# First modulation in two halves, and new instruction costs in the planner, for a two-layer hybrid-mixer and experts kernel

## The chip, the cores and the metric

The kernel runs on one core of a Trainium2 chip. The metric is the device time of one launch in microseconds (us); the time before is the median of three runs, 1281.8 us (1279.6 to 1284.72).

A core has TensorE (matrix products into PSUM), VectorE, ScalarE, GpSimd and SyncE. Each works through its own list of instructions in order and waits for the others by semaphores. In the profile they are PE (with PEld for the loading of a matmul's stationary operand), DVE, ACT, POOL and SP. SP here issues nearly all loads of weights.

## The reference, cut to what matters

The input is 512 tokens of width 1024; there are two layers. Every layer is modulated by six vectors (shift, scale and gate, twice) that come from one condition vector `c`:

```python
mod_all = einsum('bd,lde->lbe', silu(c), ada_w) + ada_b[:, None, :]
for l in range(2):
    sh1, sc1, g1, sh2, sc2, g2 = split(mod_all[l][:, None, :], 6, axis=-1)
    h = rms_norm(x, norm_mix_g[l]) * (1.0 + sc1) + sh1
    proj = h @ w_in[l]
    # four mixers of width 256 each, all fed from columns of proj:
    mix = concat([nsa(...), pool(...), rwkv7(...), dilated(...)])
    x = x + g1 * (mix @ w_out[l])
    h2 = rms_norm(x, norm_ffn_g[l]) * (1.0 + sc2) + sh2
    x = x + g2 * moe(h2)          # 16 experts, two per token
```

`ada_w` is 2 x 1024 x 6144 in float32, so one of the six vectors of one layer costs 4 MB of weights, multiplied with a single column.

## The kernel before, in words

**Modulation.** The 512 columns of half a vector, by four pieces of 256 rows, are one unit of 512 KB each (eight units to a vector). `ada_s` is the stream of these units in the order in which they are used: for layer 0 scale (v = 1), then shift (v = 0), then the rest. `ada` multiplies them: `zc` holds silu(c) as one column in a band of zeros, so that a matmul with a 32-column window of `zc` as stationary operand puts its result in row j = 2v + jj of a 32-row group (jj is the half of the vector). Four groups run side by side on TensorE, and VectorE adds all rows to `MT`, where the bias already stands (L667). `mcol` (L726) then takes rows of `MT` and turns them into columns: entry k of `A1` and `B1` is what contraction tile k of the projection is scaled and shifted by, and tiles 0 to 3 come from half 0, tiles 4 to 7 from half 1.

**The head of layer 0.** The tokens are loaded, their square sums taken (`rms`, two ScalarE passes for each of the four row tiles, L797), each row scaled by its norm, and the eight tiles of 128 columns transposed on TensorE and copied from PSUM to `hf` by ScalarE (L873, L881). Then SP is told to load the 16 units of scale and shift and two units of the projection's weights, and the main program waits for `ada` as a whole. After that follow the affine of all eight tiles (L900 on ScalarE for odd tiles, L902 on VectorE for even ones), their split into a rounded part `hH` (L903, ScalarE) and the rest `hL` (L905, VectorE), and the projection.

**Products.** Every large product is made of three matmuls in a rounded 32-bit form: high by high, high by low and low by high (`mm3`, L603 to L605). Weights are split in the same way (`split`, L555 on ScalarE and L556 on VectorE) by the streams' `presplit`, one or more units ahead. The projection runs by chunks of columns, `c0`, `c1`, `c2`, `t0`, `t1`, `t2`; a chunk takes four weight units u, each of which covers contraction tiles 2u and 2u + 1. Chunk `c0` has four column tiles, so a unit is 24 matmuls of 512 columns.

**Order.** The program is written as generators: a main one (the projections, the output projection, the experts) and side ones (the recurrent mixer, attention, pooling, modulation, routing). `_Weaver` interleaves them while the instructions are emitted, by the forecasts of `_Clock`, a small model of the engines that runs along: `cost` gives each instruction a time, `see` adds waits for data from other engines (`SEM`, 130 ns), `pass_time` forecasts TensorE's two clock levels. A side's next step is emitted once its forecast of readiness plus a lead is before TensorE's forecast time. `W.pace` sets lead and share for each stage (`PROJ`, `ATT`, `WOUT`, `MOE`). So the forecast decides in which order instructions stand on every engine, in both layers, and on the chip each engine then keeps to that order. A step that a `yield side` asks for is emitted at once, ready or not.

**Buffers.** 39 buffers of 512 KB (`G`) hold tokens, raw and split weights and most intermediate tiles; SP's loads wait until a buffer is free. PSUM has four buffers in pool `PA` and four in `PB`.

Of the kernel before, what the change touches and what calls it, by code (L numbers as in the profile page):

```python
# [210 lines left out]
class _Clock:  # L211
# [5 lines left out]
    def __init__(self, nc):  # L217
        self.free = {}
        self.acc = {}
        self.pools = {}  # L220
        self.psum = set()
        self.dma = self.mark = 0.0
        self.off = False
        self.tick, self.cols, self.cold = 0.0, 0.0, True
        self.batch, self.batch_end = set(), 0.0
        nc.push_inst_callback(self.see)
# [29 lines left out]
    @staticmethod  # L256
    def cost(eng, inst, psum):
        o = inst.outs[0]
        shape = [int(n) for _, n in o.ap]
        n = 1  # L260
        for x in shape[1:]:
            n *= x
        if eng == "PE":
            i0 = inst.ins[0]
            if inst.is_transpose:
                return 0.84 * n
            if i0.dtype == F32R and n >= 256 or i0.dtype == BF:
                return max(0.42 * n, 25.0)
            return 1.67 * max(n, shape[0])
        if eng == "DVE":  # L270
            return 65 + 1.04 * n
        if eng == "Activation":
            return (94 if psum else 180) + 0.833 * n + (94 if len(inst.outs) > 1 else 0)
        if "TensorScalar" in str(inst.opcode):
            return 100 + 3.7 * n
        return 70 + (2.25 if len(inst.ins) > 1 else 1.0) * n
# [12 lines left out]
    def see(self, inst):  # L289
        if self.off:  # L290
            return
        try:
            outs = [o for o in inst.outs if hasattr(o, "bass_ap")]
            ins = [i for i in inst.ins if hasattr(i, "bass_ap")]
            if not outs:
                return
            eng = str(inst.engine).split(".")[-1]
            rd, wr = [self.region(i) for i in ins], [self.region(o) for o in outs]
        except (AttributeError, TypeError, ValueError):
            return  # L300
        t = self.free.get(eng, 0.0)
        mine = t
        for regs, write in ((rd, False), (wr, True)):
            for name, p0, p1, lo, hi in regs:
                for q0, q1, l2, h2, end, w, by in self.acc.get(name, ()):
                    if (write or w) and by != eng and q0 < p1 and p0 < q1 and l2 < hi and lo < h2:
                        if end > t:
                            t = end
        if "DMA" in str(inst.opcode):
            self.free[eng] = mine + (1000.0 if eng == "Pool" else 50.0)  # L310
            sizes = [4 * float(np.prod([int(n) for _, n in x.ap])) for x in outs + ins]
            self.dma = max(self.dma, t + 1300.0) + min([z for z in sizes if z > 16384] or sizes) / 360.0
            end = self.dma + 500.0
        else:
            c = self.cost(eng, inst, bool(rd) and rd[0][0] in self.psum)
            if eng == "PE":
                m, q0 = int(outs[0].ap[0][1]), wr[0][1]
                kr, r0 = int(inst.ins[0].ap[0][1]), rd[0][1]
                qs = {(a, b) for a in range(r0 // 32, (r0 + kr + 31) // 32) for b in range(q0 // 32, (q0 + m + 31) // 32)}
                small = m <= 64 or kr <= 64  # L320
                self.pass_time(t)
                slow = 2 if self.cold and HAM else 1
                c *= slow
                if not small or qs & self.batch or t >= self.batch_end:
                    t = max(t, self.batch_end)
                    self.batch = qs
                    self.batch_end = t + c
                    more = c
                    if small:
                        more = min(c, 0.84 * m * slow)  # L330
                else:
                    self.batch |= qs
                    self.batch_end = max(self.batch_end, t + c)
                    more = 0.84 * m * slow
                n = 1
                for _, x in inst.outs[0].ap[1:]:
                    n *= int(x)
                n *= 1 if inst.ins[0].dtype != F32 else 2 if inst.is_transpose else 4
                self.pass_time(t + c / 2, n * int(inst.ins[0].ap[0][1]) / 128)
                self.free[eng] = t + more  # L340
            else:
                self.free[eng] = t + c
            end = t + c + self.SEM
        self.mark = max(self.mark, end)
        for regs, write in ((rd, False), (wr, True)):
            for name, p0, p1, lo, hi in regs:
                lst = self.acc.setdefault(name, [])
                if write:
                    lst[:] = [a for a in lst if not (p0 <= a[0] and a[1] <= p1 and lo <= a[2] and a[3] <= hi)]
                lst.append((p0, p1, lo, hi, end, write, None if "DMA" in str(inst.opcode) else eng))  # L350
                if len(lst) > 60:
                    del lst[:20]
        self.log[inst.name] = (t, end) if self.log is not None else None
# [86 lines left out]
def fused(ctx: ExitStack, tc: tile.TileContext, A, out, dbg=None):  # L440
# [31 lines left out]
    def TI(name, w=64, dt=F32):  # L472
        return tip.tile([128, w], dt, name=name, tag="ti")

    def PA(name):
        t_ = pa.tile([128, 512], F32, name=name, tag="a")
        K.alloc("a", NPA, t_)
        return t_
# [162 lines left out]
    def mod_rows(l):  # L641
        GP.memset(MT, 0.0)
        GP.dma_start(MT[0:12], A["ada_b"][l])
        if l + 1 < L:
            GP.dma_start(MT[12:16], A["ada_b"][l + 1, 0:4])


    ada_s = Stream([(A["ada_w"][l, 2 * v + jj, u], 512) for l, v in
                    [(0, v) for v in (1, 0, 2, 4, 3, 5)] + [(1, v) for v in (1, 0, 2, 4, 3, 5)]
                    for jj in range(2) for u in range(4)], 3, raw=True)  # L650

    def ada(l, vs, more=True):
        if more:
# [146 lines left out]
    def rms(xt, n=NT):  # L800
        ms = TI("ms", n)
        for t in range(n):
            square(xt[t], ms[:, t:t + 1])
        V.tensor_scalar(ms, ms, 1.0 / D, EPS, op0=OP.mult, op1=OP.add)
        rs_ = TI("rs_", n)
        rsqrt(ms, rs_, n)
        return rs_
# [38 lines left out]
    def layer(l, xt, mixs, moes, nmixs):  # L846
# [23 lines left out]
        def transposed(k):  # L870
# [2 lines left out]
                PE.transpose(tp[:, t * 128:(t + 1) * 128], xt[t][:, k * 128:(k + 1) * 128], ident)  # L873
            return tp

        if l == 0:
            mc = PA("mc")
            A1, B1 = TI("A1", 8), TI("B1", 8)
            for k in range(8):
                tp = transposed(k)  # L880
                SC.activation(hf[k // 2][:, k % 2], tp, AF.Copy)  # L881
            ada_s.cap = 16
            ada_s.load(16)
            mixs.load(2)
            yield W.spawn(ada(0, [(0, 1), (0, 0)], False))
            mcv = mcol(mc, 0, 4)
            V.scalar_tensor_tensor(qj(A1), mcv[:, :, 2:4], 1.0, qj(col("gmix", 0, 8)), op0=OP.add, op1=OP.mult)
            V.tensor_copy(qj(B1), mcv[:, :, 0:2])
        else:
            A1, B1 = P_.A1, P_.B1  # L890
        parts = [(hH[k // 2][:, k % 2], hL[k // 2][:, k % 2]) for k in range(8)]
        late = None
        for k in range(8):
            if l == 0:
                src = f_ = hf[k // 2][:, k % 2]
            else:
                src = transposed(k)
                f_ = HG("hf1")
            if k % 2:
                SC.activation(f_, src, AF.Identity, scale=A1[:, k:k + 1], bias=B1[:, k:k + 1])  # L900
            else:
                V.tensor_scalar(f_, src, A1[:, k:k + 1], B1[:, k:k + 1], op0=OP.mult, op1=OP.add)  # L902
            SC.activation(parts[k][0], f_, AF.Copy)  # L903
            if late:
                V.tensor_tensor(late[2], late[0], late[1].bitcast(F32), op=OP.subtract)  # L905
            late = (f_,) + parts[k]
        V.tensor_tensor(late[2], late[0], late[1].bitcast(F32), op=OP.subtract)
        hH = [hH[k // 2][:, k % 2] for k in range(8)]
        hL = [hL[k // 2][:, k % 2] for k in range(8)]
        yield  # L910
# [2 lines left out]
        def cchunk(name, evac):  # L913
            n = len(CHUNKS[name])
            ps = [PA(name) for _ in range(n // 128)]
            for u in range(4):
                wh, wl = mixs.get()
                for c in range(n // 128):
                    cs_ = slice(c * 128, (c + 1) * 128)
                    for i in range(2):  # L920
                        k = 2 * u + i
                        mm3(ps[c], wh[:, i, cs_], wl[:, i, cs_], hH[k], hL[k], k == 0, k == 7)
                    if u == 3:
                        evac(c, ps[c])
                    yield
# [1353 lines left out]
```

## Time and profile before

| what | value |
|---|---|
| median of 3 runs | 1281.8 us |
| the profiled execution | 1281.02 us, span 1279.2 us |
| mean granted TensorE clock | 0.933 of full speed |
| TensorE busy | 1096.8 us, 86% of the span |
| VectorE busy | 873.5 us, 68% |
| ScalarE busy | 587.3 us, 46% |
| GpSimd busy | 161.7 us, 13% |
| read from HBM | 213.76 MB |

The span is what the profile covers; the execution's own time is 1.8 us longer. Busy time is the union of an engine's instructions. A granted clock of 1.00 is 2.4 GHz, 0.50 is 1.2 GHz. In the trace one float32 matmul of the modulation has two records. Layer 0 lies between 0 and about 637 us, layer 1 behind it.

### The profile page before, as it was taken

How to read it: one execution, taken by the hardware profiler on the slowest of the kernel's cores; microseconds unless marked ns; L12 is line 12 of the kernel's file. 1: busy time of each engine (PE TensorE's matmuls, PEld its weight loads, DVE VectorE, ACT ScalarE, POOL GpSimd, SP SyncE). 2: the span in 40 equal slices, each digit the busy share in tenths (PEclk: the TensorE clock that was granted, in tenths of full speed). 3: DMA queues.
4: the chain of work that ended last, by engine and by line, in shares of the span. 5: the costliest groups of instructions: out<-in, count | busy, mean ns of one | idle time of the engine just before them, and what ended most of it. 6: DMA issues, size and time to landing. Idle time of an engine off the chain costs nothing. (4 is left out here: it accounts for less than half of the span.)

```text
span 1279.2 us, 21615 instructions
## 1 busy us (share of the span) xinstructions
PE 1096.8 (86%) x8150; PEld 822.5 (64%) x8150; DVE 873.5 (68%) x2200; ACT 587.3 (46%) x1088; POOL 161.7 (13%) x140
## 2 busy tenths in 40 slices
PE   4699999978999579999749879998888994899995
PEld 2487678545778467777538557784476783667774
DVE  2538866666655679999852665955685465899994
ACT  4433222346672156666551411243376431666662
POOL 2000000100001222233200000001000022213331
PEclk9799999989899789999969989998978996999998
DMA  9502111956351869999351110047431428699982
GB/s 353 191 33 83 34 37 40 348 208 258 116 182 55 332 207 323 334 351 358 116 193 35 50 67 35 21 141 274 169 121 57 158 73 324 231 326 343 353 290 37
DMA packets 68320, 232.05 MB, mean 181 GB/s; under 512 B 10580, under 2 KB 11460, under 8 KB 68208
## 3 DMA queue, kind: packets, MB, share of 16 engines
q1 hardware_dynamic: 54960, 192.18, 41.1%
q0 software_dynamic: 10368, 27.92, 7.9%
q10 hardware_dynamic: 2880, 10.49, 2.2%
q8 instruction: 67, 1.10, 0.3%
q14 instruction: 45, 0.37, 0.1%
HBM read 213.76 MB, written 25.17 MB: 187 GB/s over the span
## 5 line engine op out<-in xcount | busy, mean ns | idle before, releaser
L556 DVE TENSOR_TENSOR wl<-raw,wh 128x1024 fp32r<-128x1024 f32 (+2 forms) x254 | 299.7, 1197 | 38.3 <-ACT wh L555 35.3
L555 ACT ACTIVATE wh<-raw 128x1024 fp32r<-128x1024 f32 (+2 forms) x254 | 251.0, 1038 | 14.0 <-DMA raw<-w_out 8.1
L603 PE MATMUL gu<-wh,eh 128*128 128x512 f32 x256 | 104.8, 409 | 0.0
L605 PE MATMUL gu<-wh,el 128*128 128x512 f32 x256 | 102.6, 401 | 2.4 <-DVE el L556 1.4
L604 PE MATMUL gu<-wl,eh 128*128 128x512 f32 x256 | 101.4, 396 | 0.0
L555 ACT ACTIVATE eh<-etp 128x512 fp32r<-128x512 f32 x64 | 35.0, 595 | 114.3 <-PE etp L2039 98.5
L603 PE MATMUL c<-hH,wh 128*128 128x512 f32 x176 | 71.2, 405 | 10.7 <-ACT wh L555 10.7
L603 PE MATMUL t<-wh,hH 128*128 128x512 f32 (+1 forms) x192 | 79.9, 416 | 0.0
L604 PE MATMUL t<-wl,hH 128*128 128x512 f32 (+1 forms) x192 | 71.2, 371 | 7.8 <-DVE wl L556 7.8
L605 PE MATMUL c<-hH,wl 128*128 128x512 f32 x176 | 69.9, 397 | 2.4 <-DVE wl L556 2.4
L605 PE MATMUL t<-wh,hL 128*128 128x512 f32 (+1 forms) x192 | 70.7, 368 | 0.0
L604 PE MATMUL c<-hL,wh 128*128 128x512 f32 x176 | 69.6, 396 | 0.0
L1610 ACT ACTIVATE P<-P,mx 128x128 f32<-128x128 f32 (+3 forms) x96 | 52.7, 550 | 34.1 <-DVE mx L1607 33.9
L603 PE MATMUL dp<-wh,ahl 128*128 128x512 f32 x128 | 54.2, 423 | 15.1 <-ACT ahl L555 15.1
L605 PE MATMUL dp<-wh,ahl 128*128 128x512 f32 x128 | 54.0, 422 | 12.8 <-DVE ahl L556 12.8
L1285 POOL TENSOR_SCALAR sd<-st,pcs 128x64 f32<-128x64 f32 x28 | 10.8, 398 | 409.5 <-DVE st L1309 317.6
L605 PEld LDWEIGHTS gu<-wh,el 128*128 128x128 f32 x256 | 48.8, 191 | 17.8 <-DVE el L556 7.1
L1629 PE MATMUL ptp<-cbase,P 128*128 128x128 f32 x240 | 44.0, 314 | 15.2 <-ACT P L1622 7.7
L664 PE MATMUL ada<-raw,zc 128*32 128x512 f32 x384 | 55.1, 631 | 0.9 <-DMA raw<-ada_w 0.9
L604 PEld LDWEIGHTS gu<-wl,eh 128*128 128x128 f32 x256 | 49.2, 192 | 9.3
L603 PEld LDWEIGHTS gu<-wh,eh 128*128 128x128 f32 x256 | 49.1, 192 | 9.1 <-ACT eh L555 0.5
L2007 POOL DMA_INDIRECT ga<-h2d,idx x32 | 46.5, 1454 | 61.6 <-DVE dtw L1906 17.7
(591 smaller groups left out, 2376.0 us busy)
## 6 DMA issues: line engine op xcount, KB each, us to landing
raw<-w_gu SPq DMA_DIRECT2D x120, 512.0 KB
raw<-ada_w SPq DMA_DIRECT2D x96, 512.0 KB
raw<-w_dn SPq DMA_DIRECT2D x60, 512.0 KB
raw<-win_c SPq DMA_DIRECT2D x16, 512.0 KB
raw<-win_t SPq DMA_DIRECT2D x16, 512.0 KB
raw<-w_out SPq DMA_DIRECT2D x16, 512.0 KB
x<-x SPq DMA_DIRECT2D x8, 512.0 KB
h2d<-h SPq DMA_DIRECT2D x8, 512.0 KB
```

The source lines that it names most:

```text
L555: SC.activation(h_, src, AF.Copy)
L556: eng.tensor_tensor(l_, src, h_.bitcast(F32), op=OP.subtract)
L603: PE.matmul(o, lhsT=sh, rhs=mh, start=first, stop=False)
L604: PE.matmul(o, lhsT=sh, rhs=ml, start=False, stop=False)
L605: PE.matmul(o, lhsT=sl, rhs=mh, start=False, stop=last)
L664: PE.matmul(ps[g:g + 32], lhsT=zc[:, k, 31 - j:63 - j], rhs=raws[i // 2][:, i % 2], start=u2 == jj == 0, stop=u2 == jj == 1)
L1285: GP.tensor_scalar(sd[:, i * 64:(i + 1) * 64], st[c][:, i * 64:(i + 1) * 64], pcs[i][:, c:c + 1], 0.0, op0=OP.mult, op1=OP.add)
L1610: SC.activation(P[:, par, :n], P[:, par, :n], AF.Exp, scale=-1.0, bias=mx[:, par:par + 1], accum_out=den[:, par:par + 1])
L1629: PE.transpose(tp[:, ks_], P[:, par, ks_], ident)
L2007: GP.indirect_dma_start(out=g_, out_offset=None, in_=h2d, in_offset=bass.IndirectOffsetOnAxis(ap=info[e][0], axis=0))
```

## The change

Three things are changed. The first is the planner's costs: matmuls, ScalarE and VectorE operations get other times; an operation on VectorE or ScalarE that reads what the same engine has written waits for that write's end plus `SEM`; VectorE and GpSimd operations that read two tensors from SBUF exclude each other; a change of a matmul's tile shape costs 93 ns. The leads and shares stay.

The second is the head of layer 0. The stream `ada_s` delivers half 0 of scale and shift first, then half 1. `ada_first(jj)` multiplies one half, and `cols(jj)` makes its four columns of `A1` and `B1`. Half 0 stands in the main program: three of its four matmul groups, then the transposes of tiles 0 to 3, the split of the first weight unit, the fourth group, the columns, and the affine and split of tiles 0 to 3, in between the transposes of tiles 4 to 7. Half 1 with tiles 4 to 7 is a side, `upper`, and chunk `c0` asks for it ahead of its third unit. The copies of odd transposed tiles go to VectorE.

The third is `rms` in the head: the square sums of row tiles 1 and 3 are taken on VectorE, in one pass of 1024 columns each.

```diff
 # _Clock.cost
-                return max(0.42 * n, 25.0)
-            return 1.67 * max(n, shape[0])
+                return max(0.445 * n, 25.0)
+            return (2.05 if shape[0] <= 32 and n > 128 else 1.72) * max(n, shape[0])
         if eng == "DVE":
-            return 65 + 1.04 * n
+            return 65 + 1.04 * n + (60 if len([i for i in inst.ins if hasattr(i, "bass_ap")]) > 2 else 0)
         if eng == "Activation":
-            return (94 if psum else 180) + 0.833 * n + (94 if len(inst.outs) > 1 else 0)
+            more = len([i for i in inst.ins if hasattr(i, "bass_ap") and "const" not in i.bass_ap.tensor.name]) > 1
+            return (70 if psum else 94) + 0.833 * n + 93 * more + (93 if len(inst.outs) > 1 else 0)
...
 # _Clock.see
-                    if (write or w) and by != eng and q0 < p1 and p0 < q1 and l2 < hi and lo < h2:
+                    if (write or w) and (by != eng or w and not write and eng in ("DVE", "Activation")) and q0 < p1 and p0 < q1 and l2 < hi and lo < h2:
...
+        two = sum(r[0] not in self.psum for r in rd) > 1 and "DMA" not in str(inst.opcode)
+        if eng == "DVE" and two:
+            t = max(t, self.lock["Pool"])
+        if eng == "Pool" and two:
+            t = max(t, self.lock["DVE"])
...
+                if form != self.form:
+                    self.batch_end += 93
...
+    def ada_first(jj):
+        ps = PB("ada")
+        for v in (1, 0):
+            j = 2 * v + jj
+            for u2 in range(2):
+                raws = [ada_s.get() for _ in range(2)]
+                K.mark = max(K.last(r_.tensor.name) for r_ in raws)
+                yield
+                for i in range(4):
+                    g, k = 32 * i, 4 * u2 + i
+                    PE.matmul(ps[g:g + 32], lhsT=zc[:, k, 31 - j:63 - j], rhs=raws[i // 2][:, i % 2],
+                              start=v == 1 and u2 == 0, stop=v == 0 and u2 == 1)
+        V.tensor_tensor(MT, MT, ps, op=OP.add)
...
 # rms
-            square(xt[t], ms[:, t:t + 1])
+            if t % 2:
+                V.tensor_tensor_reduce(G("jk"), xt[t], xt[t], 1.0, 0.0, op0=OP.mult, op1=OP.add,
+                                       accum_out=ms[:, t:t + 1])
+            else:
+                square(xt[t], ms[:, t:t + 1])
...
 # head of layer 0
+            def raise_(k):
+                tp = transposed(k)
+                if k % 2:
+                    V.tensor_copy(hf[k // 2][:, k % 2], tp)
+                else:
+                    SC.activation(hf[k // 2][:, k % 2], tp, AF.Copy)
+
+            def cols(jj):
+                mcv = mcol(PB("mc"), 0, 4)
+                hs_ = slice(4 * jj, 4 * jj + 4)
+                V.scalar_tensor_tensor(A1[:, hs_], mcv[:, :, 2 + jj], 1.0, col("gmix", 4 * jj, 4), op0=OP.add, op1=OP.mult)
+                V.tensor_copy(B1[:, hs_], mcv[:, :, jj])
+
+            def upper_half():
+                yield from ada_first(1)
+                cols(1)
+                yield
+                yield from part_of(range(4, 8))
+
             ada_s.cap = 16
-            ada_s.load(16)
-            mixs.load(2)
-            yield W.spawn(ada(0, [(0, 1), (0, 0)], False))
-            mcv = mcol(mc, 0, 4)
...
+            ada_s.load(8)
+            mixs.load(2)
+            ada_s.load(12)
+            mixs.load(3)
+            ada_s.load(16)
+            mixs.load(4)
+            steps = ada_first(0)
+            for _ in range(4):
+                next(steps)
+            for k in range(4):
+                raise_(k)
+            mixs.presplit(1)
+            for _ in steps:
+                pass
+            cols(0)
+            for k, _ in enumerate(part_of(range(4)), 4):
+                raise_(k)
+            upper = W.spawn(upper_half(), front=True, lead=0)
...
 # cchunk
                 wh, wl = mixs.get()
+                if u == 2 and upper is not None:
+                    yield upper
```

`part_of(ks)` is the former loop over tiles (affine, high part, low part one tile later) for the tiles `ks`, with a `yield` after each.

## Rows read from the trace of the kernel before

**Rows 1.** Busy time by stretch: start:end, length, busy us (instructions) by engine, clock, DMA, GB/s.
```profile
0.00:46.00 46.00, 17.53 (x105) 8.69 (x106) 15.50 (x62) 21.96 (x42) 8.26 (x19) 0.91 0.95 355
...
100.00:250.00 150.00, 145.81 (x1557) 109.43 (x1556) 107.78 (x314) 43.09 (x84) 2.95 (x6) 0.99 0.28 101
250.00:372.00 122.00, 107.56 (x1030) 70.93 (x1026) 76.13 (x305) 71.16 (x202) 3.62 (x10) 0.90 0.55 198
...
454.00:637.00 183.00, 166.74 (x879) 127.54 (x877) 168.78 (x260) 119.32 (x160) 52.10 (x29) 0.98 0.83 288
...
700.00:750.00 50.00, 40.08 (x179) 26.79 (x179) 31.49 (x76) 19.19 (x28) 0.00 (x0) 0.95 0.18 61
...
870.00:1004.00 134.00, 112.08 (x1033) 77.36 (x1025) 82.93 (x328) 74.60 (x208) 4.67 (x12) 0.87 0.42 144
```

**Rows 2.** Timeline of the head: start, us, engine, line, operation [idle before <-releaser].
```profile
17.79 5.09 PE L873 MATMUL tp<-cbase,x 128*128 128x128 f32 x30 [0.35 <-ACT x L865]
...
22.81 6.13 PE L664 MATMUL ada<-raw,zc 128*32 128x512 f32 x48
...
31.73 1.05 PE L664 MATMUL ada<-raw,zc 128*32 128x512 f32 x4 [0.23 <-DMA raw<-ada_w]
...
33.01 1.05 PE L664 MATMUL ada<-raw,zc 128*32 128x512 f32 x4 [0.23 <-DMA raw<-ada_w]
34.11 0.69 DVE L667 TENSOR_TENSOR mt<-mt,ada 128x512 f32<-128x512 f32 x1 [6.82 <-PE ada L664]
...
34.85 1.05 PE L726 MATMUL mc<-cbase,mt 128*128 128x4 f32 x8 [0.79 <-DVE mt L667]
...
36.30 0.55 DVE L902 TENSOR_SCALAR hf<-hf,A,B 128x512 f32<-128x512 f32 x1
...
38.90 1.29 DVE L905 TENSOR_TENSOR hL<-hf,hH 128x512 fp32r<-128x512 f32 x2 [0.22 <-ACT hH L903]
...
45.57 0.80 PE L603 MATMUL c<-hH,wh 128*128 128x512 f32 x1 [9.67 <-ACT wh L555]
```

**Rows 3.** Busy time by stretch of 2 us in the head.
```profile
18.00:20.00 2.00, 2.00 (x11) 2.00 (x11) 0.00 (x0) 1.19 (x2) 0.00 (x0) 1.00 1.01 406
...
36.00:38.00 2.00, 0.00 (x0) 0.00 (x0) 1.20 (x4) 1.12 (x2) 0.00 (x0) 1.00 1.04 408
38.00:40.00 2.00, 0.00 (x0) 0.00 (x0) 1.78 (x4) 1.97 (x4) 0.00 (x0) 0.54 1.01 404
```

**Rows 4.** Timeline of TensorE, the first projection matmuls.
```profile
51.26 0.63 PE L603 MATMUL c<-hH,wh 128*128 128x512 f32 x1
51.69 0.46 PE L604 MATMUL c<-hL,wh 128*128 128x512 f32 x1
...
52.22 0.39 PE L603 MATMUL c<-hH,wh 128*128 128x512 f32 x1
...
59.70 0.39 PE L603 MATMUL c<-hH,wh 128*128 128x512 f32 x1
```

**Rows 5.** Groups by line and form: out<-in xcount | busy us, mean ns | idle before.
```profile
L556 DVE TENSOR_TENSOR wl<-raw,wh 128x1024 fp32r<-128x1024 f32 x238 | 286.1, 1219 | 24.7 <-ACT wh L555 21.7
L555 ACT ACTIVATE wh<-raw 128x1024 fp32r<-128x1024 f32 x238 | 239.2, 1056 | 14.0 <-DMA raw<-w_out 8.1 <-DMA raw<-w_gu 3.3 <-issue 2.4
...
L1633 DVE COPY pt<-ptp 128x512 f32<-128x512 f32 x12 | 8.2, 687 | 3.4 <-PE ptp L1629 3.4
```

**Rows 6.** Timeline of VectorE: two operations, the second reads the first's result.
```profile
726.47 0.68 DVE L996 TENSOR_TENSOR df<-vfirst,zv 128x512 f32<-128x512 f32 x1
727.19 0.69 DVE L997 TENSOR_TENSOR df<-df,vrs 128x512 f32<-128x512 f32 x1
```

**Rows 7.** Timeline of TensorE: first output projection, layer 1's first projection and output projection.
```profile
372.11 0.50 PE L603 MATMUL wo<-wh,mH 128*128 128x512 f32 x1
...
663.89 0.47 PE L603 MATMUL c<-hH,wh 128*128 128x512 f32 x1
...
1003.93 0.50 PE L603 MATMUL wo<-wh,mH 128*128 128x512 f32 x1
```

## The prediction before the run

> **What bounds the kernel now.** I read the times and the page first, then the table of busy time by stage, then the timeline of the head, then the waits of TensorE. The table by stage [rows 1] shows four kinds of stretch. In the head (0 to 46 us) TensorE works 17.5 of 46 us while the DMA share is 0.95: the loads set the pace. In the projections TensorE is nearly full. In the attention stretches (250 to 372, 870 to 1004) it loses 14.4 and 21.9 us to waits, and its mean granted clock is 0.90 and 0.87. In the experts (454 to 637) VectorE works 168.8 of 183 us and the DMA share is 0.83, so TensorE is not the only bound there.
>
> The change's hand-made part lies in the head. Its timeline [rows 2] is a chain: the last raw piece of `ada_w` lands, its matmuls start at 33.01, VectorE adds the result to `mt` at 34.11, the column matmuls start at 34.85, the first affine at 36.30, and the first projection matmul only at 45.57, after 9.67 us in which TensorE did nothing. The last two waiting groups stand 1.28 us apart (31.73, 33.01): one 512 KB piece per 1.28 us. The projection then starts at half clock: the granted clock falls from 1.00 (36 to 38 us) to 0.54 (38 to 40 us) [rows 3], and matmuls come 0.43 us apart (51.26, 51.69), after that 0.227 us (33 of them from 52.22 to 59.70) [rows 4]. The first two weight units of chunk c0 (48 matmuls, contraction tiles 0 to 3) end where the 49th matmul starts, at 59.70.
>
> **The change, part by part.** All sums are against the profiled execution's 1281.0 us (span 1279.2); the median shown is 1281.8, so 0.8 is added at the end.
>
> *Loads.* Lower-half pieces of both vectors come first (8), then two weight units, four upper pieces, one unit, four upper, one unit. Counting 1.28 us back from 33.01, the eighth piece lands at 22.8 as it does now; the first weight unit at 24.1; the last upper piece, behind three weight units that now precede it, at 33.0 + 3 x 1.28 = 36.8. The bytes are the same, the queue (SP's) is the same; so upper modulation data come 3.8 us later than now and lower data 10.2 us earlier than the whole does now.
>
> *Lower chain.* Three of the four lower matmul groups stand ahead of the first transposes on TensorE, so the transposes wait for the sixth piece (20.2) plus 1.05: 21.3. Now 30 transposes take 5.1 us [rows 2], 0.68 per tile of four, held by ScalarE's copies; with every second copy on VectorE (a copy of that shape 0.69 [rows 5]) I take 0.6 per tile: 23.7 for four tiles. The fourth group adds 1.06 (48 records in 6.13 us [rows 2], 8 per group): 24.8. The add to `mt` stands behind the low split of weight unit 0 on VectorE: unit 0 lands 24.1, ScalarE's high part 1.06, VectorE's low part 1.22 [rows 5], so the add starts at 26.3 and ends at 27.0. Column matmuls 1.1, A and B 0.36 (34.85 to 36.30 [rows 2], less the wait): first affine at 28.5. Now the high and low parts of tiles 0 and 1 are there some 3.3 us after the first affine (36.30; the second and third low parts start 38.90 [rows 2]); the copies of the upper transposes lie between them, one on ScalarE and one on VectorE, so I take 4.0: 32.5. The square sum of rows 1 and 3 moves to VectorE: two passes over 128x1024, at most about 1.22 each [rows 5], on an engine that waits there anyway; TensorE starts its transposes on pieces, not on the norm, so it gains and costs nothing. Without that cover it would cost 2.4.
>
> *Both units of the lower half.* 48 matmuls at 0.227 are 10.9 us, of which three may run before 32.5: 42.7. Two upper groups land before 32.5 (pieces at 26.6 to 30.5) and fit into the wait; two more fall in between, 2.1 us. The second add and the second column matmuls are new waits in TensorE's order: 1.05 for the columns, 0.69 for the add and up to 1.2 for a split queued ahead of it on VectorE; queued behind the columns on TensorE are the remaining c0 matmuls, which everything later waits for. I take 2.5. Sum 47.3. The upper chain, if its last group is placed soon after 36.8, has tiles 4 and 5 by about 45.8, so it doesn't end last. The third unit starts at about 47.5 instead of 59.70: **12 us gained.** Bounds: 14 if all stalls vanish (45.5), 3 if the last upper group is placed at the end of the second unit (the chain of 4.5 us is then open) and the first unit runs at half clock (24 x 0.2 = 4.8). The rope tables, a side on VectorE, share the stretch; I leave them in the 2.5.
>
> *Does the shift reach the end?* The matmuls from 52.22 on have no gap [rows 4], TensorE works 145.8 of 150 us from 100 to 250, the DMA share there is 0.28 [rows 1], and all later loads are released by buffers that TensorE frees. Nothing in the first 400 us waits for an absolute time, so I carry the 12 us through.
>
> *The planner's new costs.* They change no instruction but the order of nearly all of them, in both layers. What they correct is visible: a 512-column matmul is forecast at 0.215 (0.42 per column) and takes 0.227 [rows 4]; two VectorE operations where the second needs the first start 0.72 apart [rows 6] and were forecast at 0.60. Late forecasts of VectorE put work too early in TensorE's order, and TensorE then stands: idle 4.2, 14.4, 9.9 and 21.9 us in 100 to 250, 250 to 372, 700 to 750 and 870 to 1004 [rows 1], 50 us together. The leads and shares, which were set under the old forecast, stay. Best case: half of the 50 goes, -25. Worst case: the trace holds two orders of nearly the same work. From the first projection matmul to the first of the output projection layer 0 takes 372.1 - 45.57 = 326.5 and layer 1 takes 1003.93 - 663.89 = 340.0 [rows 2, 7]; part of the 13.5 is extra work of layer 1, so it is an upper bound of what an order is worth, for two layers 27. Between -25 and +27 I take -3, near nothing: the correction points the right way, its size isn't shown. The lock between VectorE and GpSimd hardly matters where GpSimd works 3 us of 150 [rows 1].
>
> Sum: 1281.0 - 12 - 3 = 1266.0; with 0.8 for the median **1267 us**.
>
> *A rule against it.* The granted clock is 1.00 during the transposes (18 to 20 us) and still from 36 to 38, and falls after TensorE has had no instruction since 35.9 [rows 2, 3]. The Trainium skill says of transposes ("TensorE: Matmul & The Clock Gate", Part 4: PE-mode transpose) that they do not count as busy for the clock the way matmuls do. The order after has 32 transposes with only short matmul groups between 21 and 31 us, so by that rule the first lower unit would meet the half clock; no run here yet shows it, since now a dense matmul group follows the transposes at once. What this would cost is the rival "half clock" below.
>
> **Rivals.**
> - *Half clock.* The lower units start at 0.43 per matmul. For it: sparse matmuls between 21 and 32 us. Against it: the groups paced by the loads, 1.05 us in 1.28, left the clock at 1.00 until 36 to 38 us [rows 2, 3]. At 14 slow matmuls as now [rows 4] 2.8 us are lost, at all 48 it is 9.6 us: 1270 to 1276.
> - *The wait moves.* The upper chain ends last at the third unit, because its add and splits queue on VectorE or its last group is placed late. For it: VectorE has splits, rope and both adds there. 4 to 6 us of the 12 remain: 1273 to 1275.
> - *The order takes it all* (the other side). The new forecasts make side work be issued later, the unchanged leads then come too late, and TensorE waits more in projections and attention of both layers. It decides from 6 us per layer on. At 13.5 per layer: 1281.8 - 12 + 27 = 1297. For it: nothing else in the planner was set anew. Against it: the new costs are nearer to the rows.
> - *The order gives much.* Half of TensorE's 50 us of waits go: 1281.8 - 12 - 25 = 1245.
> - *The halves do nothing*: the lower part is forced behind the upper in TensorE's order, no gain in the head, 1279.
>
> **Numbers.** The forecast (1260 to 1273) 0.42; half clock 0.10; the wait moves 0.08; the order gives much 0.16; head gain eaten to within measurement 0.14, of it the idle halves 0.03; order takes more 0.10. A measurement of this kernel tells changes above some 0.5%, 6.4 us. Faster: 0.42 + 0.10 + 0.08 + 0.16 = 0.76; same 0.14; slower 0.10. Low end 1249: three quarters of "gives much" is inside. High end 1283: it holds the two late rivals and the eaten gain, and leaves out the slower cases. The likeliest case's own range is 1260 to 1273.
>
> **What would show it.** Right: the first c matmul before 33 us, the 49th at 46 to 49, its wait under 2 us; the last `ada` matmul at about 37 to 39; granted clock 1.00 from 24 to 50; two `mt` adds, near 26.5 and 40. Wrong in the head: a TensorE wait of over 3 us ended by VectorE (`hL`, `mt`) before the 49th matmul, or 0.43 us spacing. The planner's part is read from the same two intervals, 326.5 and 340.0: taken from the 49th c matmul on in layer 0, and whole in layer 1. If the second moves by over 10 us either way, the -3 was the failed step; if the experts' stretch moves by over 5, the carry-through was.

## The result and the profile after

The change ran in 1260.55 us (median of four runs, 1255.66 to 1272.69) against 1280.7 us before (1279.08 to 1284.72): a ratio of 0.9859, 95% interval [0.9821, 0.9897], or 18 us (13 to 23). A second measurement of the same kernel, among the experiments, gave 1257.09 us and 0.9809 [0.9784, 0.9833]. The forecast was 1267, with 1249 to 1283 as its range.

The profiled execution is the longest of the four (1272.69 us), so it understates the gain. Its page, part 1: busy time, share of the span, instructions.

```profile
span 1270.9 us, 21609 instructions
...
PE 1106.8 (87%) x8158; PEld 822.9 (65%) x8158; DVE 874.7 (69%) x2208; ACT 581.7 (46%) x1076; POOL 167.6 (13%) x140
```

TensorE is busy 10 us longer than before, with eight more records (the second set of column matmuls) and no lower mean clock (0.935 against 0.933). What differs is how much of its work meets the half clock: counted from the trace, 114 us of TensorE's busy time fall into half clock, against 102 before, where more of the half clock fell into waits. The second profile below (69 us) shows the same order with less of it.

The head, timeline of the changed kernel (columns as in [rows 2], which it answers):

```profile
23.40 1.06 PE L677 MATMUL ada<-raw,zc 128*32 128x512 f32 x8
...
25.39 1.23 DVE L569 TENSOR_TENSOR wl<-raw,wh 128x1024 fp32r<-128x1024 f32 x1 [1.19 <-ACT wh L568]
26.53 0.68 DVE L679 TENSOR_TENSOR mt<-mt,ada 128x512 f32<-128x512 f32 x1
...
27.27 1.87 PE L755 MATMUL mc<-cbase,mt 128*128 128x4 f32 x8 [2.81 <-DVE mt L679]
...
29.00 3.65 PE L906 MATMUL tp<-cbase,x 128*128 128x128 f32 x16
...
29.44 0.55 DVE L923 TENSOR_SCALAR hf<-hf,A,B 128x512 f32<-128x512 f32 x1
...
34.14 0.50 PE L616 MATMUL c<-hH,wh 128*128 128x512 f32 x1
34.48 0.39 PE L617 MATMUL c<-hL,wh 128*128 128x512 f32 x1
34.71 0.39 PE L618 MATMUL c<-hH,wl 128*128 128x512 f32 x1
...
42.26 1.07 PE L677 MATMUL ada<-raw,zc 128*32 128x512 f32 x8
43.41 0.69 DVE L679 TENSOR_TENSOR mt<-mt,ada 128x512 f32<-128x512 f32 x1 [3.88 <-PE ada L677]
...
44.16 1.05 PE L755 MATMUL mc<-cbase,mt 128*128 128x4 f32 x8 [0.84 <-DVE mt L679]
```

The lower chain runs as forecast: the add to `mt` at 26.53 (forecast 26.3), the first affine at 29.44 (28.5). The first projection matmul starts at 34.14 instead of 45.57. Then TensorE's own timeline:

```profile
50.64 0.39 PE L616 MATMUL c<-hH,wh 128*128 128x512 f32 x1
...
51.32 0.39 PE L616 MATMUL c<-hH,wh 128*128 128x512 f32 x1
53.71 0.50 PE L617 MATMUL c<-hL,wh 128*128 128x512 f32 x1 [2.00 <-DVE hL L926]
...
54.72 0.63 PE L617 MATMUL c<-hL,wh 128*128 128x512 f32 x1
55.14 0.63 PE L618 MATMUL c<-hH,wl 128*128 128x512 f32 x1
```

The matmul at 50.64 is the 49th of chunk c0 (59.70 in [rows 4]). Four matmuls later TensorE waits 2.0 us for the low part of tile 5, and the next nine or so come at half clock. The 96th, the last of c0, starts at 65.2 against 70.4 before: of the 9.1 us at the 49th, 5.2 are left.

**Two runs of one order.** A second profile of the changed kernel (experiment e4) has the same instructions in the same order, took 1256.07 us, and starts its instructions from 20 to 27 us within 0.05 us of the first one's (0.4 us before); behind that they part. Its head, timeline of TensorE:

```profile
27.22 1.05 PE L755 MATMUL mc<-cbase,mt 128*128 128x4 f32 x8 [2.81 <-DVE mt L679]
28.14 1.94 PE L906 MATMUL tp<-cbase,x 128*128 128x128 f32 x16
30.33 1.07 PE L677 MATMUL ada<-raw,zc 128*32 128x512 f32 x8 [0.25 <-ACT hf L938]
31.33 0.50 PE L616 MATMUL c<-hH,wh 128*128 128x512 f32 x1
```

The wait of 2.81 us is the same; but the column matmuls take 1.05 and not 1.87 us, the transposes 1.94 and not 3.65, and the projection starts at 31.33. Busy time by stretch (columns as in [rows 3]), first the run above, then e4:

```profile
24.00:26.00 2.00, 0.46 (x8) 0.00 (x0) 0.81 (x2) 1.06 (x1) 0.00 (x0) 1.00 1.05 418
26.00:28.00 2.00, 0.73 (x4) 0.73 (x4) 1.21 (x2) 0.00 (x0) 0.00 (x0) 0.74 1.00 401
28.00:30.00 2.00, 2.00 (x11) 2.00 (x11) 0.78 (x3) 0.00 (x0) 0.00 (x0) 0.50 1.05 416
```
```profile
26.00:28.00 2.00, 0.78 (x7) 0.78 (x8) 1.17 (x2) 0.00 (x0) 0.00 (x0) 1.00 1.02 408
28.00:30.00 2.00, 2.00 (x19) 1.84 (x18) 0.95 (x4) 0.84 (x2) 0.00 (x0) 1.00 1.04 410
```

In the long run the granted clock fell to 0.50 during that wait, in e4 it stayed at 1.00. The two later stretches of the mixers, below, show the same on a larger scale.

**Where the time went.** Three parts of each profile are compared: the head up to the 96th c matmul; M0, from there to layer 0's first output-projection matmul; M1, from layer 1's first c matmul to its first output-projection matmul. All the rest is one number. Busy time by stretch for M0 and M1; the first figure after the length is TensorE's busy time, the last three are clock, DMA share and GB/s. Before, first profile, then before, second profile (e9), the change, the change again (e4):

```profile
70.40:372.10 301.70, 283.06 (x2711) 203.75 (x2709) 194.77 (x631) 126.86 (x301) 7.60 (x17) 0.95 0.37 136
663.90:1003.90 340.00, 304.35 (x2744) 224.25 (x2741) 208.74 (x648) 137.54 (x317) 7.69 (x18) 0.94 0.28 99
```
```profile
69.30:372.20 302.90, 282.09 (x2711) 202.21 (x2709) 194.87 (x631) 126.52 (x301) 7.59 (x17) 0.96 0.38 135
665.40:1003.50 338.10, 301.79 (x2745) 222.85 (x2742) 208.99 (x648) 137.25 (x317) 7.69 (x18) 0.95 0.29 99
```
```profile
65.20:373.60 308.40, 289.32 (x2712) 205.88 (x2710) 195.08 (x631) 126.14 (x301) 9.37 (x17) 0.93 0.37 133
663.50:997.80 334.30, 307.39 (x2745) 226.68 (x2743) 207.51 (x648) 136.85 (x317) 8.53 (x18) 0.94 0.28 101
```
```profile
60.90:361.60 300.70, 279.01 (x2711) 200.74 (x2710) 195.06 (x631) 125.97 (x301) 9.38 (x17) 0.97 0.38 136
652.20:981.00 328.80, 300.28 (x2744) 221.67 (x2742) 207.54 (x648) 136.87 (x317) 8.53 (x18) 0.96 0.29 102
```

Length less busy time is TensorE's idle time. Time at half clock is 2 x (1 - clock) x length, good to about 3 us because the clock has two decimals. With both, for all kernels that were profiled (us):

| kernel | 49th c | 96th c | M0 length, idle, half clock | M1 length, idle, half clock | rest | span |
|---|---|---|---|---|---|---|
| before | 59.7 | 70.4 | 301.7, 18.6, 30 | 340.0, 35.6, 41 | 567.1 | 1279.2 |
| before again (e9) | 58.6 | 69.3 | 302.9, 20.8, 24 | 338.1, 36.3, 34 | 569.4 | 1279.7 |
| the change | 50.6 | 65.2 | 308.4, 19.1, 43 | 334.3, 26.9, 40 | 563.0 | 1270.9 |
| the change again (e4) | 48.0 | 60.9 | 300.7, 21.7, 18 | 328.8, 28.5, 26 | 563.7 | 1254.1 |
| new costs alone (e1) | 59.5 | 70.2 | 310.9, 22.2, 44 | 330.6, 29.6, 26 | 562.3 | 1274.0 |
| halves alone (e2) | 51.9 | 62.7 | 299.6, 17.9, 24 | 333.9, 32.7, 33 | 567.0 | 1263.2 |
| rope later (e3) | 50.5 | 61.2 | 296.3, 18.9, 18 | 334.2, 26.9, 40 | 562.6 | 1254.3 |
| rope later again (e11) | 50.8 | 61.5 | 296.1, 18.9, 12 | 329.2, 28.4, 26 | 562.3 | 1249.1 |
| split later (e6) | 49.5 | 62.5 | 297.1, 19.4, 12 | 329.8, 26.2, 33 | 563.3 | 1252.7 |
| both later (e8) | 48.0 | 58.7 | 303.1, 20.8, 30 | 330.4, 29.7, 26 | 565.6 | 1257.8 |
| loads at 410 (e5) | 51.2 | 61.9 | 306.7, 23.8, 25 | 329.9, 28.1, 26 | 566.2 | 1264.7 |
| old matmul costs (e12) | 48.9 | 60.2 | 299.5, 20.3, 24 | 326.6, 24.2, 33 | 569.0 | 1255.3 |
| no own wait (e7) | 49.8 | 60.5 | 314.7, 27.1, 38 | 356.9, 43.2, 57 | 568.4 | 1300.5 |

Read from this, the first profile's 8.3 us are: head -5.2, M0 +6.7, M1 -5.7, rest -4.1. The second profile's 25.1 us are: head -9.5, M0 -1.0, M1 -11.2, rest -3.4. The 16.8 us between the two runs lie in the head (4.3), M0 (7.7) and M1 (5.5); idle times agree within 2.6 us, and TensorE's busy times differ by 10.3 us in M0 and 7.1 in M1, as the half-clock time does (43 against 18, 40 against 26). Idle time in M1 fell from 36 to 27 or 28.5; M0's did not fall.

### The profile page after: what moved, and what is told of

It reads as the page before. It is cut to its first block, busy times and chain, and to the rows that moved or that the text cites. A ratio compares the mean times of both kernels' runs of the same rounds, so it can differ in the third digit from the quotient of the medians.

```text
span 1270.9 us, 21609 instructions
## 1 busy us (share of the span) xinstructions
PE 1106.8 (87%) x8158; PEld 822.9 (65%) x8158; DVE 874.7 (69%) x2208; ACT 581.7 (46%) x1076; POOL 167.6 (13%) x140
## 5 line engine op out<-in xcount | busy, mean ns | idle before, releaser
L1353 POOL TENSOR_SCALAR sd<-st,pcs 128x64 f32<-128x64 f32 x28 | 13.4, 491 | 413.2 <-DVE st L1377 315.5
L1678 ACT ACTIVATE P<-P,mx 128x128 f32<-128x128 f32 (+3 forms) x96 | 52.7, 551 | 27.1 <-DVE mx L1675 20.2
L616 PEld LDWEIGHTS gu<-wh,eh 128*128 128x128 f32 x256 | 48.9, 191 | 9.0 <-ACT eh L568 0.5
L616 PE MATMUL wo<-wh,mH 128*128 128x512 f32 x128 | 52.4, 409 | 0.0
```

The lines of the kernel that those rows point to most:

```text
L616: PE.matmul(o, lhsT=sh, rhs=mh, start=first, stop=False)
L1353: GP.tensor_scalar(sd[:, i * 64:(i + 1) * 64], st[c][:, i * 64:(i + 1) * 64], pcs[i][:, c:c + 1], 0.0, op0=OP.mult, op1=OP.add)
L1678: SC.activation(P[:, par, :n], P[:, par, :n], AF.Exp, scale=-1.0, bias=mx[:, par:par + 1], accum_out=den[:, par:par + 1])
```

## The experiments

Each was timed in five rounds beside the kernel before (e9 in one), and profiled.

**e1, the new costs alone, and e2, the halves alone.** e1 is the kernel before with the new `_Clock`; e2 is the change with the old `_Clock`:

```diff
 # e2, against the change
-                return max(0.445 * n, 25.0)
+                return max(0.42 * n, 25.0)
...
-                    if (write or w) and (by != eng or w and not write and eng in ("DVE", "Activation")) and q0 < p1 and p0 < q1 and l2 < hi and lo < h2:
+                    if (write or w) and by != eng and q0 < p1 and p0 < q1 and l2 < hi and lo < h2:
```

> The planner's new costs alone, on the head of before. Theory (head and order both pay): the profile of the change shows the 49th c matmul 9.1 us earlier and the 96th 5.2 us earlier than before, so the head carries 5 to 9 of the some 20 us of the medians and the new costs the rest: 1266 to 1271. Rival A (the head pays all): 1278 to 1283, as before. Rival B (any new order gains or loses by chance): anywhere from 1265 to 1290, and the two parts alone do not add up to the whole.

> The halves, the copies on VectorE and the square sums on VectorE, with the planner's old costs. Theory: first c matmul near 34 us, the 49th at 48 to 54, total 1271 to 1276. Rival A: 1258 to 1265, as the whole change. Rival B: the shift of the head by itself makes a new order downstream too, so layer 1's stretch from first c to first output-projection matmul differs from 340.0 by more than 3 us although no cost of it was changed.

Measured: e1 1272.04 us, ratio 0.9921 [0.99, 0.9943]; e2 1262.45 us, ratio 0.9843 [0.982, 0.9866]. Both parts pay, and e1's rival "the head pays all" falls. But both sizes were missed: the halves alone give 19 us in the medians, which is the band of e2's rival A, though only 7.7 of them are there at the 96th matmul. The rest appears downstream. M1 is 333.9 against 338.1 to 340.0, with 3 us less idle time, although none of its costs was changed. Its order of TensorE instructions differs from before's in some 4% of the rows when the two lists are aligned, M0's in 13%: the halves shift the planner's forecast times, and so the interleaving behind them. e2's rival B is right in that.

The new costs alone do nothing in the head (70.2), take 6 to 7 us of idle time from M1 and 5 to 7 us from the rest, and give 8 to 9 us back in M0, where its profile has 44 us of half clock. Some of the rest's gain lies between output projection and experts: this stretch takes 82.3 us in layer 0 and 81.9 in layer 1 before, 80.5 and 80.6 in e1, 80.7 and 80.7 in e4. TensorE's waits in layer 0's, before and then e4 (us in total, times, longest):

```profile
PE rps L1890 <- DVE mb L1885: 5.5, 1, 5.5
PE etp L2039 <- DMA ga<-h2d,idx: 4.2, 1, 4.2
PE lg L1789 <- ACT xT L1785: 3.3, 1, 3.3
```
```profile
PE rps L1958 <- DVE mb L1953: 4.7, 1, 4.7
...
PE lg L1857 <- ACT xT L1853: 2.4, 2, 1.7
PE etp L2107 <- DMA ga<-h2d,idx: 2.2, 1, 2.2
PE tp L1852 <- DVE x L1985: 1.7, 1, 1.7
```

The three waits of before are shorter by 3.7 us together (2.9 in e1), but the last line is a new one, in e1 too, which takes 1.7 of that back. The two stretches are some 3 us of the rest's gain; where the others come from is open.

**e4, the change again.**

> The change itself again, since its four runs lie between 1255.7 and 1272.7 and the profiled one was the longest. Theory: the order of instructions is the same in each run, and the runs differ in where TensorE's clock falls (mean granted clock 0.935 in the long run, 0.941 to 0.950 in the others): the median is 1257 to 1264, long runs have the lower clock, and the stretches that differ between the two profiles are those with a granted clock under 0.95. Rival: the runs differ in a wait on a load, with the same clock.

Measured: 1257.09 us (1254.3 to 1260.4). The theory held: the profiles differ where the clock differs, as shown above. Over the nine runs of both measurements the longest has the lowest clock (1272.69 us at 0.935); the other eight have 0.941 to 0.953 and 1254.3 to 1261.5.

**e9, before again.**

> The kernel before itself, for a second profile: how much do its stretches differ between runs of the same order. Theory: head and idle times repeat within 1 us (49th c matmul at 59.7, idle 18.6 and 35.6 us in the two mixer stages), and only the half-clock time differs (30 and 41 us now). Rival: the idle time of 35.6 us in layer 1 was itself luck, and comes out under 31.

Measured: 1281.03 us, ratio 1.0002. Idle times repeat to 2.2 us in M0 and 0.7 in M1, so the 36 us of M1 are the order's and no luck. The head came 1.1 us earlier; this and M0's idle time differ a little more than the 1 us expected.

**e7, without the wait for what the same engine wrote.**

```diff
-                    if (write or w) and (by != eng or w and not write and eng in ("DVE", "Activation")) and q0 < p1 and p0 < q1 and l2 < hi and lo < h2:
+                    if (write or w) and by != eng and q0 < p1 and p0 < q1 and l2 < hi and lo < h2:
```

> The change without one of the planner's new costs: an operation on VectorE or ScalarE no longer waits, in the forecast, for what the same engine wrote before. The order of TensorE's matmuls in layer 1's mixer stage is then about as far from the change's as that of before is. Theory: this cost is what takes TensorE's idle time in layer 1's stage from first c to first output-projection matmul from 33 to 36 us (old costs) to 27 to 30 (new): without it the idle time is 32 to 36 us again, the stretch from output projection to experts goes back from 80.7 to 82.3, and the total is 1262 to 1268, like the halves alone. Rival: the other costs (matmul, ScalarE) do it, idle 27 to 30, total 1254 to 1260.

Measured: 1300.25 us, ratio 1.0136 [1.0109, 1.0163], 40 to 43 us slower than the change and 1.4% slower than before. I had the direction and not the size: idle time in M1 goes to 43.2, above that of the old costs. Waits of TensorE in M1, e7 and then e4:

```profile
PE ptp L1697 <- ACT P L1690: 7.8, 4, 3.1
PE s L1672 <- DVE mx L1675: 6.2, 4, 4.8
```
```profile
PE ptp L1697 <- ACT P L1690: 2.3, 3, 1.4
...
PE s L1672 <- DVE mx L1675: 1.7, 4, 0.8
```

Attention's chain from scores over VectorE's minimum and ScalarE's exponential to the transposes is issued too early: these two lines are 10 of the 15 us of idle time that M1 gained against e4. A likely reason why it is worse than before: with ScalarE's costs cut (180 to 94 ns of fixed time for SBUF operands) and no own wait, the forecast of such chains is more optimistic than the old one was. No run has the own wait alone on top of the old costs, nor ScalarE's old costs with the own wait, so this is argued and not shown.

**e12, TensorE's old costs.**

```diff
-                return max(0.445 * n, 25.0)
-            return (2.05 if shape[0] <= 32 and n > 128 else 1.72) * max(n, shape[0])
+                return max(0.42 * n, 25.0)
+            return 1.67 * max(n, shape[0])
...
-                    self.batch_end += 93
+                    self.batch_end += 0
```

> The change with TensorE's old costs (0.42 and 1.67 ns per column, nothing for a change of shape); the costs of VectorE and ScalarE and the wait for what the same engine wrote stay new. Leaving out that wait made the kernel 43 us slower than the change, by TensorE's idle time (27.1 and 43.2 us in the two mixer stages, now 19 to 22 and 27 to 30) and half-clock time. Theory A: the own wait alone carries the planner's gain, so idle stays at 26 to 30 us in layer 1 and the total at 1254 to 1264. Theory B: the costs only work as a set, one piece alone unbalances TensorE's forecast against VectorE's: idle over 32 us in layer 1, total over 1270.

Measured: 1257.09 us, ratio 0.9829 [0.9806, 0.9852]; idle in M1 24.2. The time and M1's idle time go with theory A: TensorE's new costs are not what pays. That the own wait alone does is not shown by it, since the other costs of VectorE and ScalarE stay new. Only the rest (569.0) is back at the old figure.

**e3 and e11, the rope tables later.** In the changed kernel the upper half's low parts stand behind other work. VectorE, timeline:

```profile
45.40 1.21 DVE L569 TENSOR_TENSOR wl<-raw,wh 128x1024 fp32r<-128x1024 f32 x1
46.53 0.54 DVE L923 TENSOR_SCALAR hf<-hf,A,B 128x512 f32<-128x512 f32 x1
46.99 0.17 DVE L786 TENSOR_SCALAR kf<-ang 128x40 f32<-128x40 f32 x1
...
49.05 0.18 DVE L797 COPY rcs<-rcs 128x40 f32<-128x40 f32 x1 [0.30 <-ACT rcs L796]
49.15 0.68 DVE L926 TENSOR_TENSOR hL<-hf,hH 128x512 fp32r<-128x512 f32 x1
51.37 1.23 DVE L569 TENSOR_TENSOR wl<-raw,wh 128x1024 fp32r<-128x1024 f32 x1 [1.55 <-ACT wh L568]
...
52.97 1.47 DVE L926 TENSOR_TENSOR hL<-hf,hH 128x512 fp32r<-128x512 f32 x2
```

A weight split, then the rope operations, then `hL` of tile 4 at 49.15; then VectorE waits for ScalarE's part of another weight split (51.37), and only behind that comes `hL` of tile 5, at 52.97. The edit:

```diff
-        if l == 0:
-            W.spawn(rope_tables())
...
         at["c0"].done = True
+        if l == 0:
+            W.spawn(rope_tables())
```

> The change, with the side of the rope tables started behind chunk c0 instead of ahead of it. In the profile of the change TensorE waits 2.0 us at 51.3 for a low part of the upper half that stands behind rope operations on VectorE and ScalarE, and then runs ten matmuls at half clock. Theory: without the rope operations the low part of tile 5 is there before 51, that wait and the half clock go, the 96th c matmul comes at 61 to 62 instead of 65.2, and the total falls by 3 to 4 us against the change. Rival: the splits of weight units 2 and 3 alone delay the upper half as much (the wait stays over 1 us) and the total is the change's within 2 us.

> The fastest version so far, the change with the rope tables behind chunk c0, again, beside the others: 1254.6 us in its first five rounds, the change 1257.1 and 1260.6. Theory: it is faster than the change by the wait taken away, 1252 to 1257, and its idle times repeat (17.6, 18.9, 26.9 us in the head and the two mixer stages). Rival: the difference was where the clock fell, and it comes out at 1257 to 1261, like the change.

Measured: 1254.56 us, 0.9778 [0.9753, 0.9803], and 1254.15 us, 0.9811 [0.9784, 0.9839]. The wait is gone in both, and the 96th matmul comes at 61.2 and 61.5 although the clock had fallen at 27 us in both. It isn't the rope operations alone that have moved: in e3 VectorE starts the low part of tile 5 at 49.04 and the second weight split at 51.88, behind it, so the run does not tell the two apart. Against the change's two results this is 3 to 6 us in the medians. Both intervals overlap that of e4 (e3's does not reach the first measurement's): the head is mended as expected, the total is not shown to be faster than the change.

**e6, the first split behind the columns, and e8, both mends.**

```diff
-            mixs.presplit(1)
             for _ in steps:
                 pass
             cols(0)
+            mixs.presplit(1)
```

> The change, with the split of the first weight unit emitted behind the lower half's columns instead of ahead of its add to mt. In both profiles of the change TensorE waits 2.8 us (24.4 to 27.2) for that add, which stands behind the split's low part on VectorE; in one of them the granted clock falls to half during that wait and stays there until 33, in the other it does not. Theory: the add starts at 24.5 instead of 26.5, the wait shrinks to 0.8 us, the clock stays at 1.00 through the head, the first c matmul comes at 30 to 32, and since the order downstream is the same but for this piece, the total is 1253 to 1258 with a narrower spread than the change's. Rival: the low part of the weight unit is then late by the same 2 us (TensorE waits for wl at the first unit instead), and nothing is gained.

> Both mends of the head together, rope tables behind chunk c0 and the split of the first weight unit behind the lower columns. Theory: neither the wait of 2.8 us near 25 nor the one of 2.0 us near 51 is left, the clock stays up, the 96th c matmul comes at 58 to 60 (now 70.4 before, 60.9 to 65.2 in the change), and the median is 1249 to 1254, some 5 us under the change. Rival: what is taken from the head is given back in layer 0's mixer stage, whose length (296 to 311 us so far) follows its half-clock time and not the head: median 1254 to 1260.

Measured: e6 1258.38 us (0.9836 [0.9814, 0.9857]), e8 1259.54 us (0.9837 [0.9821, 0.9853]). The head obeys in part: e6's first c matmul is at 28.9, but its clock falls all the same, at 31.5, and its 96th is at 62.5; e8's 96th is at 58.7, the earliest of all, without half clock up to there. The totals do not obey: neither beats the change, and e6's rival is partly right. Its waits up to 64 us:

```profile
PE c L617 <- DVE hL L926: 2.5, 3, 2.0
PE mc L755 <- DVE mt L679: 1.7, 2, 0.9
PE c L616 <- ACT hH L924: 1.2, 2, 0.8
```

The wait moves to `hH` and `hL` (not to `wl`, as the rival had it), and the one at tile 5 stays. In e8 M0 takes 303.1 us with 30 us of half clock: its rival, "given back in M0", is what came out.

**e5, the loads' forecast at 410 GB/s.**

```diff
-            self.dma = max(self.dma, t + 1300.0) + min([z for z in sizes if z > 16384] or sizes) / 360.0
+            self.dma = max(self.dma, t + 1300.0) + min([z for z in sizes if z > 16384] or sizes) / 410.0
```

> The change with the planner's forecast of the load rate at 410 instead of 360 GB/s; the trace moves one 512 KB piece per 1.28 us, 410 GB/s. In the change the last upper matmul group stands at 42.3 in TensorE's order, though its piece lands at about 37. Theory: the group moves to 37 to 39.5, the second add to mt ends before 41 instead of 44.1, the wait of 2 us for the low part of tile 5 is gone and the 96th c matmul comes at 59 to 62. The order of layer 0's mixer stage becomes another one too (9% of its rows), so the total may go either way by some 5 us: 1250 to 1264. Rival: the group's place follows TensorE's forecast and not the loads', and stays past 41.

Measured: 1263.74 us, ratio 0.986 [0.984, 0.988]. The last upper group and the second add in e5 (timelines of TensorE and VectorE):

```profile
40.15 1.07 PE L677 MATMUL ada<-raw,zc 128*32 128x512 f32 x8
42.03 1.05 PE L755 MATMUL mc<-cbase,mt 128*128 128x4 f32 x8 [0.81 <-DVE mt L679]
```
```profile
41.29 0.69 DVE L679 TENSOR_TENSOR mt<-mt,ada 128x512 f32<-128x512 f32 x1 [1.32 <-PE ada L677]
```

The group moved only from 42.3 to 40.2, short of the 39.5 that I expected, and the add comes 2.1 us earlier. In the order it moved further: it stands behind 12 matmuls of c0 instead of 24, and c0 itself began 1.8 us later (35.97). The wait for tile 5 is gone, and the head gains what was forecast (96th at 61.9, though at half clock from 28 us). The total gains nothing: M0's length (306.7) lies between the change's two, with more idle time (23.8) than either.

## Why the prediction was right or wrong

- **Loads, lower chain.** Right. The transposes began at 21.47 (forecast 21.3), the add at 26.53 (26.3), the first affine at 29.44 (28.5); the square sums and copies on VectorE cost nothing on this path. One term was not what its row gives: a matmul group by 6.13 us for six is 1.02 and not 1.06, but 1.06 is what it took.
- **The third unit at 47.5, 12 us gained.** 48.0 in the run where the clock held (11.7 us), 50.6 where it fell (9.1). "The first c matmul before 33 us" holds for the first of these runs (31.3) alone.
- **"The upper chain doesn't end last."** Wrong: this step of the working failed. The last upper group stands at 42.3 (39.6 in e4) instead of soon after 36.8. It is placed behind 24 matmuls of c0, for the planner's loads are slower than the trace's: with 410 GB/s it is placed behind 12 (e5). Then two weight splits and the rope operations put the low part of tile 5 at 52.97. My 2.5 us for waits covers the waits at the adds, but not this one, which begins behind the 52nd matmul. So the rival "the wait moves" is true by 2.0 us, and at the 96th matmul 9.5 or 5.2 of the 12 are left.
- **Half clock, the rival.** Not as it was stated: in neither profile do the lower units run at 0.43 us per matmul. Their first ones follow each other by 0.23 (34.48, 34.71), and 0.43 is met only behind the wait for tile 5. But the clock does fall ahead of them: in the first profile in TensorE's wait at 24.5 to 27.3, and it is back by 34, so that columns, transposes and one upper group are slow and the 49th matmul comes 2.6 us later than in e4, just under the low end of the rival's price (2.8). The rival was given 0.10, yet a fall is the rule: of the ten profiles of kernels with the halves, eight have a granted clock of 0.50 that begins between 26 and 32 us; only e4 and e8 stay at 1.00. The Trainium skill's sentence on transposes ("TensorE: Matmul & The Clock Gate", Part 4: PE-mode transpose), that they don't count as busy in the same way, does not decide this: in e4 the same 32 transposes stand around the same wait and the clock stays at 1.00, which is not what the prediction drew from it.
- **The shift reaches the end.** Right in direction, too small in size, and for a reason that the prediction didn't have: it treated the head as a pure shift. e2 shows that it also changes the planner's forecast times and with them M0's and M1's order; alone it is worth 19 us in the medians and not 12. The experts, the sign named for this step, did not move: from the first to the last `gu` matmul layer 0 takes 177.1 us before, 177.4 and 177.5 after.
- **New costs, -3.** The term was too small: -9 alone (e1), about -5 on top of the halves (1262.45 to 1257.09). The bounds of -25 and +27 were far too careful on the good side and not on the bad: e7, one line away, is 40 us slower. By the prediction's own sign (layer 1's interval of 340.0 moves by over 10) the -3 failed in the second profile (328.8) and not in the first (334.3). The mechanism named (VectorE's results forecast too early, TensorE stands) fits e7 and e12; which of VectorE's and ScalarE's new costs pay was not tested one by one. Alone, the new costs took 6 to 7 us of idle time from M1 (e1) and none from M0; with the halves M1 lost 7 to 9.
- **The sum.** The forecast of 14 to 15 us became 18 and 24 in two measurements. That it lies so near is in part luck, as its errors offset each other: in the second profile the head kept 9.5 of its 12 us at the 96th matmul, while M1 gave 11.2 and the rest 3.4, where the sum had 3 for both; in the first the head kept 5.2, M1 and the rest gave 9.8, and M0 took 6.7 back at half clock. The parts alone add to 28; 24 was measured on the same chip. Whether the difference of 4 us is real stays open: the intervals are about 3 us each. Open too is why the clock falls in one run of an order and not in another.

## What to carry to other kernels

A forecasting scheduler makes every edit a global one: a faster head, or a single cost, changes the order of everything behind it, and that was worth as much here as the edit itself; its costs are to be tested one by one (without one of them the change lost 40 us, without three others nothing) and the result read stage by stage. Where one list of instructions can meet two clocks, compare idle times and half-clock times, not lengths: idle time repeated within 3 us when the total moved by 17. In a chain that is cut in halves, look at what stands ahead of the second half on every engine it uses: here that brought back a wait of 2.0 us behind the first half.

## What was not expected of the hardware

The same order of instructions with the same wait of 2.81 us kept TensorE at 2.4 GHz in one run and dropped it to 1.2 GHz in another, and over both mixer stages the time at half clock was 44 us in one run and 83 us in the other: 1256.07 against 1272.69 us. The runs of before on record spread over 1276 to 1288 us, at a mean clock of 0.930 to 0.940 (48 runs); that the change spreads wider rests on its one run of 1272.69 us, since its other eight lie within 1254.3 to 1261.5.
